# Hybrid pooling and SSD layer on one core: scan exponents and sample-state scaling on ScalarE, one state product on GpSimd, two output weights split in earlier stages

## The chip, the cores and the metric

The kernel runs on one core of a Trainium2 chip. The metric is device time in microseconds, from launch to the end of the last instruction, as the median of several executions. Times of single instructions come from one profiled execution of the kernel before, recorded by the hardware profiler. Engines are named as the profile names them: PE is TensorE (PEld its weight loads), DVE is VectorE, ACT is ScalarE, POOL is GpSimd, and SP is the queue of the engine that issues nearly all DMAs.

## The reference, cut to what matters

One layer of a decoder trunk: a SwiGLU FFN, a token mixing with two branches (multi-scale causal pooling and a Mamba-2 SSD scan, merged by gates), and a second SwiGLU FFN. There are 1024 prompt tokens and 8 x 8 sample tokens, D_MODEL 1024, D_FF 2816, 32 SSD heads of 64 channels in 4 groups, state 128, chunks of 128 tokens. All inputs are float32.

```python
def ssd_scan(x, dt, A, bm, cm, h0):
    ...
    a_cs = jnp.cumsum(dtr * A.reshape(G, R), axis=2)
    ...
    seg = jnp.where(causal, acs_t[..., :, None] - acs_t[..., None, :], -jnp.inf)
    decay = jnp.exp(seg)
    cb = jnp.einsum('bclgn,bcsgn->bcgls', cr, br)
    y_diag = jnp.einsum('bcgrls,bcsgrp->bclgrp', cb[:, :, :, None] * decay, xdt)
    ...
    def step(h, inp):
        s_c, d_c = inp
        return h * d_c[..., None, None] + s_c, h
    ...

def token_mixing(...):
    proj = hn @ w_in
    ...
    branch_pool = pool_mix(u_ext, T, out_pos0, pool_w_group, pool_scale) @ pool_w_out
    ...
    branch_ssd = y @ ssd_w_out
    gates = jax.nn.sigmoid(gate_logits.astype(f32)).reshape(Bsz, T, N_BRANCHES, D_MODEL)
    merged = (gates[:, :, 0] * branch_pool.astype(f32) + gates[:, :, 1] * branch_ssd.astype(f32)).astype(hn.dtype)
    return merged @ w_o, new_pool, new_conv, new_ssm
```

The decay is exp(a_l - a_s) on and below the diagonal of a chunk. Above the diagonal the exponent is positive and the result is multiplied by zero, so the kernel limits it to zero first.

## The kernel before

**Layout and precision.** Activations lie with channels on the 128 partitions and tokens along the row, in two halves: half 0 is 512 prompt tokens, half 1 is 512 prompt tokens and the 64 sample tokens. A float32 product is made of three passes over split operands, hi x hi, lo x hi and hi x lo, where hi is the operand rounded for the fast matmul and lo the rest. `split` (line 352) makes hi on ScalarE (line 354) and lo on VectorE (lines 356, 358). Weights come in chunks of 512 x 128 (256 KB).

**Weights.** `load_w` (line 270) loads a raw chunk (`wraw`, line 290), makes `wh` on ScalarE (293) and `wl` on VectorE (294). With `keep` it also stores both parts to DRAM (298), for half 1 to load them (283) without a split. `part` (line 304) is a generator that does the same ahead of time: it loads a chunk as `pr` (308), waits PART_W, splits it (354, 356), stores `ph` and `pr` (314, 315), waits PART_PACE, and takes the next one. `parted` holds what has been stored, and `load_w` looks there first. Before the change 52 chunks go through `part`: during FFN 1, twelve of its output weight, twelve of FFN 2's input weight and sixteen of w_o; during FFN 2, twelve of its output weight. `pool_w_out` (16 chunks) and `ssd_w_out` (32 chunks) are split in the mixing stage by half 0, with `keep`.

**Stages.** FFN 1 (to about 800 us of the span), the input projection (to 1510), the mixing stage (to 2220), FFN 2. FFN input and projection multiply pairs of weight tiles by the seven products of a Strassen-Winograd scheme (`wino`, line 466); each product is done for half 0 and half 1, its PSUM bank is read by ScalarE or VectorE and, for three of the four later products on that bank, is used again one product after. The sums of weights are made on GpSimd (436), their parts on ScalarE (442) and VectorE (443).

**The mixing stage** does, in this order on TensorE: pool branch of half 0 and of half 1 (`pgm`, `pbp`), then for each half the SSD output product group by group (`pso`), the merge, and the output projection (`pwo`). Beside them runs the scan as a generator, `scan`, through `ssd_group` for half 0 groups 0 to 3 and half 1 groups 0 to 3; a chunk is prepared by `ssd_a` (decay matrix `ab`, transposes), used by `ssd_b` one chunk later, and its state is made by `ssd_st`. Half 1 has a fifth chunk per group with the sample tokens, whose states `h` are loaded, transposed, updated and stored in 8 units per group.

**What sets the order.** Generators are called chains. Each `yield x` says that the chain continues when x more units have passed on `pe[0]`, a running estimate of TensorE's time in us, which is raised at every matmul as the program is written out. STEP is the distance between the steps of the scan for half 0 and half 1. Where an output is needed before its chain has come that far, `scanned` runs the chain on without waiting. The tile framework then orders the instructions of each engine and inserts the waits. Each engine executes its queue strictly in order, and so does SP with its DMAs: a store that waits for its data holds the loads behind it.

Of the kernel before, what the change touches and what calls it, by code (L numbers as in the profile page):

```python
# [12 lines left out]
ALU = mybir.AluOpType  # L13
# [29 lines left out]

STEP = (5.0, 4.0)
STEP_S = 1.0
# [10 lines left out]
HP, HP_ST = 40, 0  # L56
PART_AT, PART_W, PART_PACE = 20.0, 4.0, 3.0


@with_exitstack  # L60
def tile_hybrid_pool_ssd_macaron(
# [71 lines left out]
    def start(gen, delay=0.0):  # L133
        c = Chain(gen, delay)
        chains.append(c)
        return c
# [990 lines left out]
    def in_proj(prep):  # L1127
# [23 lines left out]
        c = poster[0] = start(worker())  # L1151
        work.append(sample_hist())
        for i in range(N_GATE[0], 16, 2):
            proj_pair("g", i, i + 1, both)
# [4 lines left out]
        ahead_d = []  # L1159
        for k in range(2):  # L1160
            ahead_d.append(load_d(0, k))
        for i in range(N_GATE[1], N_GATE[0], 2):
            proj_pair("g", i, i + 1, both[1:])
        last[0] = True
        for c_ in dts + [c]:
            finish(c_)
# [29 lines left out]
    out01 = [(kb, min(4, NFF - kb), m * P) for m in (0, 1) for kb in range(0, NFF, 4)]  # L1196

    def side():
        yield from part(ffn1_w_out[0], out01)
        yield from part(ffn2_w_in[0], [(kb, 4, c0 + ff * P) for ff in range(N_PLAIN[0]) for kb in (0, 4) for c0 in (0, FF)])  # L1200
        yield from part(w_o[0], [(kb, 4, m * P) for m in range(KD) for kb in (0, 4)])

# [19 lines left out]
    def pool_branch(h):  # L1222
# [20 lines left out]
        for m in range(KD):  # L1243
            t = act((P, N), name="t0")
            dma(t, gd[h][m])
            pb = dense(pool_w_out[0], 0, KD, m * P, [(h, fh, fl)], name="pbp", keep=True)[0]
            for pt, (a, b) in zip(pb, PIECES[h]):
# [38 lines left out]
    def ssd_a(h, g, c, Bf, Cf, xs4, dts):  # L1286
# [46 lines left out]
        for q, ab in enumerate(abs_):  # L1333
# [4 lines left out]
            for i in range(hq):  # L1338
                V.tensor_scalar(ab[:L, i, :], ab[:L, i, :], acs[:L, hc + q * hq + i : hc + q * hq + i + 1], 0.0,
                                op0=ALU.subtract, op1=ALU.min)  # L1340
            S.activation(ab[:L], ab[:L], AF.Exp)
            V.tensor_tensor(ab[:L], ab[:L], cbm[:L, :L].unsqueeze(1).broadcast_to([L, hq, L]), op=ALU.mult)
        return abs_, xp, xd, ea, btok, L, tok

    def ssd_b(h, g, c, a, hold, Cf, y4, dts):
# [8 lines left out]
        if smp:  # L1354
# [22 lines left out]
            for i, (pr, bh) in enumerate(units):  # L1377
                if i + 3 < len(units):
                    h0s[i + 3] = load(units[i + 3])
                hTs[pr], h0 = turn(h0s[i]), h0s.pop(i)  # L1380
                yield STEP_S
                gp = g * 4 + pr
                pn = psum("ps", "pnew")
                mm(pn, xd[bh][0][:, pr * P : (pr + 1) * P], xd[bh][1].rearrange("p b n -> p (b n)"))
                for b in range(4):
                    V.scalar_tensor_tensor(h0[:, b, :], h0[:, b, :], cdp[0][:, gp, bh * 4 + b : bh * 4 + b + 1],
                                           pn[:, b * P : (b + 1) * P], op0=ALU.mult, op1=ALU.add)
                dst = new_ssm_s[0, bh * 4 : bh * 4 + 4, 2 * gp : 2 * gp + 2].rearrange("b h p n -> (h p) b n")
# [34 lines left out]
    def ssd_st(h, g, c, a, dts):  # L1423
# [10 lines left out]
        with tc.high_priority(HP_ST):  # L1434
            if hold is None:
                S.copy(hn_, pst)
            else:
                V.tensor_tensor(hn_.rearrange("p (h d) -> p h d", d=HD), hold.rearrange("p (h d) -> p h d", d=HD),
                                cd[:, hc : hc + HPG].unsqueeze(2).broadcast_to([P, HPG, HD]), op=ALU.mult)
                V.tensor_tensor(hn_, hn_, pst, op=ALU.add)  # L1440
# [123 lines left out]
    def merge(h, acc):  # L1564
# [18 lines left out]
        for m in range(KD):  # L1583
            pb = dense(ssd_w_out[0], (NG - 1) * 4, 4, m * P, [yn], name="pso", keep=True)[0]
            while merged[0] <= m:
# [162 lines left out]
```

## Time and profile before

| | us |
|---|---|
| median of three timed runs | 2989.28 |
| lowest and highest of them | 2986.2, 2989.44 |
| the profiled execution | 2982.28 |
| its span, first to last instruction | 2980.5 |
| PE busy in the span | 2842.1 |
| mixing stage, 1520 to 2220 of the span: PE, VectorE, ScalarE, GpSimd busy | 624.9, 543.8, 267.2, 156.1 |

The mean granted clock of TensorE over the span is 0.982 of full speed. Times in the profile are us from the start of the span, durations in groups are ns. Matmuls are pipelined, so two can be counted as running at once, and a busy PE is not yet PE at its peak. A wait is put down to what ended last.

### The profile page before, as it was taken

Reading aid. Unit: us, or ns where it says so; the run is one execution under the profiler, and the core shown is the slowest. Engines: PE = TensorE matmul, PEld = TensorE weight load, DVE = VectorE, ACT = ScalarE, POOL = GpSimd, SP = SyncE. Lnnn points to the kernel's source line nnn. Section 1 sums busy time; section 2 is a strip of 40 time slices with the busy share of each in tenths; the row PEclk is TensorE's granted clock in tenths of the full one; section 3 lists DMA queues with packets and bytes.
Section 4 is the critical chain, followed back from the end, with each engine's and each line's share of the span. In section 5 each row is a group of like instructions: output and inputs, shape, how many; then the busy total and the mean of one; then the engine's idle time right before and its main releaser. Section 6 shows DMA issues by size and latency. Waiting matters only on the chain. (4 is left out here: it accounts for less than half of the span.)

```text
span 2980.5 us, 51010 instructions
## 1 busy us (share of the span) xinstructions
PE 2842.1 (95%) x18494; PEld 2580.8 (87%) x18494; DVE 1838.0 (62%) x3255; ACT 1264.6 (42%) x2592; POOL 963.4 (32%) x983
## 2 busy tenths in 40 slices
PE   7999999999999999999988998798999999999998
PEld 6999998789889989999876876577999999997898
DVE  6555556424564677696957798888666554453432
ACT  5444445323344555455543354334133444443422
POOL 5444444000233455464411221222125444440000
PEclk9999999999999999999998999899999999999999
DMA  4575554865343242323388888776674432236652
GB/s 133 162 225 180 173 159 149 270 192 177 100 124 110 88 136 87 125 96 119 109 277 285 280 266 253 231 248 196 226 244 157 155 110 80 77 94 220 210 161 73
DMA packets 521884, 503.78 MB, mean 169 GB/s; under 512 B 36628, under 2 KB 366216, under 8 KB 521624
## 3 DMA queue, kind: packets, MB, share of 16 engines
q1 hardware_dynamic: 521616, 500.52, 52.9%
q8 instruction: 145, 2.38, 0.3%
q14 instruction: 107, 0.88, 0.1%
q10 hardware_dynamic: 16, 0.00, 0.0%
HBM read 349.19 MB, written 151.44 MB: 168 GB/s over the span
## 5 line engine op out<-in xcount | busy, mean ns | idle before, releaser
L162 PE MATMUL pw<-X,wh 128*128 128x288 f32 (+1 forms) x2484 | 623.3, 330 | 13.7 <-ACT v L559 4.9
L162 PE MATMUL pw<-X,wl 128*128 128x288 f32 (+1 forms) x1644 | 472.8, 288 | 1.9 <-DVE wl L443 1.9
L162 PEld LDWEIGHTS pw<-X,wh 128*128 128x128 f32 x2484 | 418.1, 189 | 52.7 <-ACT v L559 5.8
L162 PE MATMUL pw<-hl,wh 128*128 128x512 f32 x1072 | 389.5, 398 | 1.1 <-DVE t L563 1.1
L443 DVE TENSOR_TENSOR wl<-s,wh 128x512 fp32r<-128x512 f32 x288 | 220.8, 767 | 213.6 <-ACT wh L442 192.5
L162 PE MATMUL pw<-hi,wh 128*128 128x288 f32 x1120 | 330.7, 295 | 1.0 <-ACT t L595 0.8
L162 PE MATMUL pw<-lo,wh 128*128 128x288 f32 x1120 | 329.7, 294 | 0.0
L162 PE MATMUL pw<-hi,wl 128*128 128x288 f32 x1120 | 329.6, 294 | 0.0
L294 DVE TENSOR_TENSOR wl<-wraw,wh 128x512 fp32r<-128x512 f32 x244 | 172.1, 707 | 253.4 <-ACT wh L293 247.5
L162 PEld LDWEIGHTS pw<-X,wl 128*128 128x128 f32 x1644 | 310.7, 189 | 2.5 <-DVE wl L443 2.5
L436 POOL TENSOR_TENSOR s<-wraw,wraw 128x512 f32<-128x512 f32 x144 | 204.3, 1418 | 314.1 <-DVE wl L443 223.5
L293 ACT ACTIVATE wh<-wraw 128x512 fp32r<-128x512 f32 x244 | 148.1, 609 | 365.7 <-PE po L162 239.2
L162 PE MATMUL pw<-hl,wl 128*128 128x256 f32 x1072 | 298.8, 279 | 1.2 <-DVE wl L443 1.2
L443 DVE TENSOR_TENSOR wl<-wraw,wh 128x512 fp32r<-128x512 f32 x216 | 163.9, 759 | 143.1 <-ACT wh L442 138.7
L442 ACT ACTIVATE wh<-s 128x512 fp32r<-128x512 f32 x288 | 181.1, 629 | 144.3 <-PE pw L162 141.6
L162 PEld LDWEIGHTS pw<-hl,wh 128*128 128x128 f32 x1072 | 201.2, 188 | 37.1 <-DVE t L563 1.4
L162 PEld LDWEIGHTS pw<-hi,wh 128*128 128x128 f32 x1120 | 210.0, 188 | 13.2 <-ACT t L595 1.6
L162 PE MATMUL po<-hh,wh 128*128 128x288 f32 (+1 forms) x800 | 210.6, 323 | 4.3 <-ACT hh L354 4.2
L162 PE MATMUL po<-hr,wh 128*128 128x288 f32 (+1 forms) x800 | 211.1, 323 | 0.2 <-DVE hr L356 0.2
L162 PE MATMUL po<-hh,wl 128*128 128x288 f32 (+1 forms) x800 | 210.6, 322 | 0.0
L162 PEld LDWEIGHTS pw<-lo,wh 128*128 128x128 f32 x1120 | 210.1, 188 | 0.0
L162 PEld LDWEIGHTS pw<-hi,wl 128*128 128x128 f32 x1120 | 210.1, 188 | 0.0
(383 smaller groups left out, 6256.1 us busy)
## 6 DMA issues: line engine op xcount, KB each, us to landing
wraw<-in_ffn_w_in_dram SPq DMA_DIRECT2D x188, 256.0 KB
wraw<-in_w_in_dram SPq DMA_DIRECT2D x144, 256.0 KB
wh<-part SPq DMA_DIRECT2D x140, 256.0 KB
wl<-part SPq DMA_DIRECT2D x140, 256.0 KB
wraw<-in_ffn_w_out_dram SPq DMA_DIRECT2D x120, 256.0 KB
ab<-acsd SPq DMA_DIRECT2D x64, 256.0 KB
hd<-g SPq DMA_DIRECT2D x44, 288.0 KB
part<-ph SPq DMA_DIRECT2D x48, 256.0 KB
```

The costliest lines, as they stand in the source:

```text
L162: T.matmul(out, lhsT, rhs, start=start, stop=stop, skip_group_check=free)
L293: S.activation(wh, raw, AF.Copy)
L294: V.tensor_tensor(wl, raw, wh.bitcast(F32), op=ALU.subtract)
L436: G.tensor_tensor(t, a, b, op=op)
L442: S.activation(wh, a, AF.Copy)
L443: V.tensor_tensor(wl, a, wh.bitcast(F32), op=ALU.subtract)
```

## The change

1. In `ssd_a` the clamp `min(ab - acs, 0)` per head on VectorE becomes `relu(-ab + acs)` on ScalarE with the sum as bias, and the exponential takes scale -1.
2. In `ssd_b`, for the sample states, ScalarE scales the four 128 x 128 blocks of `h` by the decay, and VectorE adds `pnew` in one instruction of 512 columns, in place of four fused instructions on VectorE.
3. In `ssd_st` the product of the running state and the chunk's decay goes from VectorE to GpSimd; the addition of `pst` stays on VectorE.
4. `pool_w_out` goes through `part` during FFN 1, after w_o; `ssd_w_out` goes through it during the projection, as a chain of its own that starts 2 units into it. The mixing stage asks for no `keep` any more, so both halves load stored parts.
5. `part` is started 6 units into an FFN's main loop, not 20, and its two waits are 2.5 and 1.5, not 4 and 3.
6. STEP goes from (5.0, 4.0) to (5.4, 4.3), and four d tile pairs of the pool branch, not two, are loaded at the projection's end.

```diff
-STEP = (5.0, 4.0)
+STEP = (5.4, 4.3)
...
-PART_AT, PART_W, PART_PACE = 20.0, 4.0, 3.0
+PART_AT, PART_W, PART_PACE = 6.0, 2.5, 1.5
...
         work.append(sample_hist())
+        split_so = start(part(ssd_w_out[0], so_chunks), 2.0)
...
-        for k in range(2):
+        for k in range(4):
             ahead_d.append(load_d(0, k))
...
-        for c_ in dts + [c]:
+        for c_ in dts + [split_so, c]:
             finish(c_)
...
+    so_chunks = [(g * 4, 4, m * P) for g in range(NG) for m in range(KD)]
...
-        yield from part(w_o[0], [(kb, 4, m * P) for m in range(KD) for kb in (0, 4)])
+        for w in (w_o[0], pool_w_out[0]):
+            yield from part(w, [(kb, 4, m * P) for m in range(KD) for kb in (0, 4)])
...
-            pb = dense(pool_w_out[0], 0, KD, m * P, [(h, fh, fl)], name="pbp", keep=True)[0]
+            pb = dense(pool_w_out[0], 0, KD, m * P, [(h, fh, fl)], name="pbp")[0]
...
             for i in range(hq):
-                V.tensor_scalar(ab[:L, i, :], ab[:L, i, :], acs[:L, hc + q * hq + i : hc + q * hq + i + 1], 0.0,
-                                op0=ALU.subtract, op1=ALU.min)
-            S.activation(ab[:L], ab[:L], AF.Exp)
+                S.activation(ab[:L, i, :], ab[:L, i, :], AF.Relu, bias=acs[:L, hc + q * hq + i : hc + q * hq + i + 1], scale=-1.0)
+            S.activation(ab[:L], ab[:L], AF.Exp, scale=-1.0)
...
                 hTs[pr], h0 = turn(h0s[i]), h0s.pop(i)
+                gp = g * 4 + pr
+                for b in range(4):
+                    S.activation(h0[:, b, :], h0[:, b, :], AF.Copy, scale=cdp[0][:, gp, bh * 4 + b : bh * 4 + b + 1])
                 yield STEP_S
...
-                for b in range(4):
-                    V.scalar_tensor_tensor(h0[:, b, :], h0[:, b, :], cdp[0][:, gp, bh * 4 + b : bh * 4 + b + 1],
-                                           pn[:, b * P : (b + 1) * P], op0=ALU.mult, op1=ALU.add)
+                hv = h0.rearrange("p b n -> p (b n)")
+                V.tensor_tensor(hv, hv, pn, op=ALU.add)
...
-                V.tensor_tensor(hn_.rearrange("p (h d) -> p h d", d=HD), hold.rearrange("p (h d) -> p h d", d=HD),
+                G.tensor_tensor(hn_.rearrange("p (h d) -> p h d", d=HD), hold.rearrange("p (h d) -> p h d", d=HD),
...
-            pb = dense(ssd_w_out[0], g * 4, 4, m * P, [yn], name="pso", keep=True)[0]
+            pb = dense(ssd_w_out[0], g * 4, 4, m * P, [yn], name="pso")[0]
```

Three places in the order of the engines' queues follow. A row has line, operation, out<-in and shape; x4 means four like it in a row.

ScalarE in the scan, in the SSD output of half 0, before. `ab` is half of a chunk's decay matrix, `ea` the decay of the old state, `btok` the transposed B, `acc` the sum of the SSD output:

```order
L1559 COPY acc_3575_19725<-pso_19683 128x512
L293 ACTIVATE wh_19872<-wraw_19871 128x512
L1321 COPY btok_19757<-pcb_19752 128x128
L1337 ACTIVATE ea_19764<-ab_19718 64x256 x2
L1337 ACTIVATE ea_19764<-ab_19720 64x256 x2
L1559 COPY acc_3591_19784<-pso_19727 128x512
L1341 ACTIVATE ab_19718<-ab_19718 128x512
L293 ACTIVATE wh_19931<-wraw_19930 128x512
L1341 ACTIVATE ab_19720<-ab_19720 128x512
```

The same place with the change (its lines are numbered up to four higher):

```order
L1563 COPY acc_3738_19906<-pso_19858 128x512
L1341 ACTIVATE ea_19937<-ab_19892 64x256
L1325 COPY btok_19930<-pcb_19925 128x128
L1341 ACTIVATE ea_19937<-ab_19892 64x256
L1343 ACTIVATE ab_19892<-ab_19892,dts_17889 128x128 x4
L1341 ACTIVATE ea_19937<-ab_19894 64x256
L1344 ACTIVATE ab_19892<-ab_19892 128x512
L1341 ACTIVATE ea_19937<-ab_19894 64x256
L1343 ACTIVATE ab_19894<-ab_19894,dts_17889 128x128 x4
L1563 COPY acc_3749_19962<-pso_19908 128x512
L1344 ACTIVATE ab_19894<-ab_19894 128x512
```

The weight's `wh` (L293) is gone from the queue, and two times four Relus (L1343) stand ahead of the exponentials (L1344).

SP in the SSD output of half 0, before, where `wraw` is a raw weight chunk and `part` the stored halves of one:

```order
L298 DMA part_20251<-wl_20246 128x512
L298 DMA part_20341<-wh_20336 128x512
L298 DMA part_20342<-wl_20337 128x512
L298 DMA part_20399<-wh_20394 128x512
L298 DMA part_20457<-wh_20452 128x512
L290 DMA wraw_20613<-in_ssd_w_out_dram 128x4x128
L290 DMA wraw_20651<-in_ssd_w_out_dram 128x4x128
L298 DMA part_20570<-wh_20565 128x512
L290 DMA wraw_20732<-in_ssd_w_out_dram 128x4x128
L1304 DMA ab_20286<-acsd_116 128x512
```

With the change:

```order
L283 DMA wh_20616<-part_11294 128x512
L283 DMA wl_20618<-part_11295 128x512
L283 DMA wh_20641<-part_11360 128x512
L283 DMA wl_20643<-part_11361 128x512
L1510 DMA bc_20439<-cv_21_165 128x576
L283 DMA wh_20727<-part_11434 128x512
L283 DMA wl_20729<-part_11435 128x512
L1308 DMA ab_20533<-acsd_116 128x512
L1308 DMA ab_20535<-acsd_116 128x512
```

No load stands behind a store of a weight any more; each chunk has two loads.

SP in FFN 1 beside the parts, before, where `pr` is a chunk to be split and `wraw` a chunk of the weight that is being multiplied:

```order
L308 DMA pr_4651<-in_w_o_dram 128x4x128
L462 DMA wraw_5078<-in_ffn_w_in_dram 128x4x128
L314 DMA part_4701<-ph_4698 128x512
L315 DMA part_4702<-pr_4651 128x512
L308 DMA pr_4749<-in_w_o_dram 128x4x128
L462 DMA wraw_5080<-in_ffn_w_in_dram 128x4x128
L314 DMA part_4798<-ph_4795 128x512
L315 DMA part_4799<-pr_4749 128x512
L462 DMA wraw_5082<-in_ffn_w_in_dram 128x4x128
L462 DMA wraw_5323<-in_ffn_w_in_dram 128x4x128
```

With the change:

```order
L308 DMA pr_3274<-in_w_o_dram 128x4x128
L462 DMA wraw_3719<-in_ffn_w_in_dram 128x4x128
L314 DMA part_3311<-ph_3308 128x512
L315 DMA part_3312<-pr_3274 128x512
L308 DMA pr_3342<-in_w_o_dram 128x4x128
L308 DMA pr_3411<-in_w_o_dram 128x4x128
L314 DMA part_3377<-ph_3374 128x512
L315 DMA part_3378<-pr_3342 128x512
L462 DMA wraw_3721<-in_ffn_w_in_dram 128x4x128
L314 DMA part_3447<-ph_3444 128x512
L315 DMA part_3448<-pr_3411 128x512
L462 DMA wraw_3723<-in_ffn_w_in_dram 128x4x128
```

Between two loads of `wraw` there is now up to a whole chunk of `pr` with its two stores, and some loads of `pr` stand ahead of the stores of the chunk before.

More of the change, by code (lines that the diff above doesn't have):

```diff
@@ L1380, in ssd_b @@
                 hTs[pr], h0 = turn(h0s[i]), h0s.pop(i)
+                gp = g * 4 + pr
+                for b in range(4):
+                    S.activation(h0[:, b, :], h0[:, b, :], AF.Copy, scale=cdp[0][:, gp, bh * 4 + b : bh * 4 + b + 1])
                 yield STEP_S
-                gp = g * 4 + pr
                 pn = psum("ps", "pnew")
                 mm(pn, xd[bh][0][:, pr * P : (pr + 1) * P], xd[bh][1].rearrange("p b n -> p (b n)"))
-                for b in range(4):
-                    V.scalar_tensor_tensor(h0[:, b, :], h0[:, b, :], cdp[0][:, gp, bh * 4 + b : bh * 4 + b + 1],
-                                           pn[:, b * P : (b + 1) * P], op0=ALU.mult, op1=ALU.add)
+                hv = h0.rearrange("p b n -> p (b n)")
+                V.tensor_tensor(hv, hv, pn, op=ALU.add)
                 dst = new_ssm_s[0, bh * 4 : bh * 4 + 4, 2 * gp : 2 * gp + 2].rearrange("b h p n -> (h p) b n")
@@ L1583, in merge @@
         for m in range(KD):
-            pb = dense(ssd_w_out[0], (NG - 1) * 4, 4, m * P, [yn], name="pso", keep=True)[0]
+            pb = dense(ssd_w_out[0], (NG - 1) * 4, 4, m * P, [yn], name="pso")[0]
             while merged[0] <= m:
```

## The prediction

> **What bounds the kernel now.** I read the busy shares first, then the windows by stage, then in the worst stage who waits for whom. The page's first part gives each engine's share of the span:
>
> ```profile
> PE 2842.1 (95%) x18494; PEld 2580.8 (87%) x18494; DVE 1838.0 (62%) x3255; ACT 1264.6 (42%) x2592; POOL 963.4 (32%) x983
> ```
>
> TensorE sets the time, so a gain can only come where it idles. The windows (PE, PEld, DVE, ACT and POOL busy us, granted clock, DMA share, GB/s): first FFN 1, the projection's gate part and its first convolutions, and FFN 2 with part tiles; then the mixing stage whole and in five pieces.
>
> ```profile
> core 0: us, PE busy (x) PEld busy (x) DVE busy (x) ACT busy (x) POOL busy (x), PEclk, DMA share, GB/s
> 100.00:500.00 400.00, 398.74 (x2695) 375.12 (x2694) 226.70 (x377) 188.38 (x414) 176.70 (x167) 1.00 0.56 177
> 860.00:1020.00 160.00, 160.00 (x1095) 150.29 (x1094) 80.69 (x138) 75.35 (x151) 59.87 (x64) 1.00 0.34 102
> 1020.00:1100.00 80.00, 77.89 (x516) 72.06 (x516) 70.86 (x117) 43.71 (x95) 45.13 (x53) 1.00 0.40 128
> 1520.00:1600.00 80.00, 61.62 (x301) 45.23 (x300) 51.77 (x108) 30.76 (x61) 13.78 (x10) 0.88 0.91 300
> 1600.00:1740.00 140.00, 133.61 (x917) 118.65 (x916) 109.97 (x241) 60.36 (x127) 28.74 (x23) 0.96 0.85 280
> 1740.00:1960.00 220.00, 187.55 (x1132) 141.29 (x1130) 192.25 (x403) 90.70 (x182) 55.95 (x46) 0.94 0.79 250
> 1960.00:2040.00 80.00, 66.65 (x451) 54.18 (x452) 64.38 (x155) 33.10 (x70) 17.82 (x15) 0.88 0.67 214
> 2040.00:2220.00 180.00, 175.48 (x1386) 168.86 (x1386) 125.45 (x239) 52.30 (x100) 39.83 (x32) 1.00 0.72 235
> 2310.00:2410.00 100.00, 98.85 (x662) 92.74 (x661) 55.14 (x88) 46.13 (x98) 47.08 (x44) 1.00 0.50 157
> ...
> 1520.00:2220.00 700.00, 624.91 (x4180) 528.21 (x4179) 543.81 (x1144) 267.22 (x538) 156.13 (x125) 0.94 0.78 254
> ```
>
> FFN 1 idles 1.3 us in 400. The mixing stage idles 75.1 in 700 and pays again through the clock: PE busy times (1 - clock) is 7.4, 5.3, 11.3, 8.0 and 0 us in the five pieces, 32 together. Idle plus clock by piece: 25.8 (pool branch, half 0; DMA share 0.91), 11.7 (pool, half 1), 43.7 (SSD output, half 0; VectorE 87% busy), 21.4 and 4.5. That is all there is to win here, some 107 us.
>
> The view of waits (who waits, for whom: us in total, times, longest) names the causes. TensorE's in the third piece:
>
> ```profile
> PE pst L162 <- DVE xd L1329: 4.2, 4, 2.5
> ...
> PE pso L162 <- DVE wl L294: 3.3, 3, 1.1
> PE pso L162 <- ACT wh L293: 3.2, 2, 2.7
> ```
>
> Those of SP's own queue, over the whole stage:
>
> ```profile
> SPq L283 <- PE pso L162: 92.9, 31, 15.5
> SPq L298 <- ACT wh L293: 47.4, 23, 6.5
> SPq L298 <- DVE wl L294: 44.3, 25, 12.5
> ```
>
> And one such wait in the timeline (start and length in us, in brackets the idle time before it and what ended it):
>
> ```profile
> 1843.90 0.32 SPq L298 DMA_DIRECT2D part<-wl  x1
> ...
> 1844.75 2.39 SPq L290 DMA_DIRECT2D wraw<-in_ssd_w_out_dram  x4
> ...
> 1849.21 0.63 ACT L293 ACTIVATE wh<-wraw 128x512 fp32r<-128x512 f32 x1 [1.91 <-DMA wraw<-in_ssd_w_out_dram]
> ...
> 1849.89 2.08 PE L162 MATMUL pso<-yhl,wh 128*128 128x512 f32 x4 [2.69 <-ACT wh L293]
> ```
>
> SP issues in order. The store of a split weight (L298) stands until VectorE has made it, the raw loads (L290) stand behind it, so ScalarE gets its chunk late and TensorE stops 2.69 us. So three things press on this stage at once: VectorE's time, SP's order and the bytes.
>
> **The change part by part.** The groups that price it, by line and shape (out<-in, count | busy us, mean ns of one | idle before, and what ended it):
>
> ```profile
> L1339 DVE TENSOR_SCALAR ab<-ab,dts 128x128 f32<-128x128 f32 x256 | 59.4, 295 | 10.0 <-ACT ea L1337 8.6
> ...
> L1339 DVE TENSOR_SCALAR ab<-ab,dts 64x64 f32<-64x64 f32 x32 | 6.2, 242 | 0.3
> ...
> L294 DVE TENSOR_TENSOR wl<-wraw,wh 128x512 fp32r<-128x512 f32 x56 | 42.5, 764 | 10.6 <-ACT wh L293 9.6 <-DMA wraw<-in_pool_w_out_dram 1.0
> ...
> L1386 DVE SCALAR_TENSOR_TENSOR h<-h,cdp,pnew 128x128 f32<-128x128 f32 x128 | 35.1, 344 | 10.5 <-PE pnew L162 8.5 <-issue 1.1 <-PE ph0T L166 0.8
> ...
> L1438 DVE TENSOR_TENSOR hst<-hst,dts 128x512 f32<-128x512 f32 x28 | 20.4, 729 | 0.0
> ...
> L1440 DVE TENSOR_TENSOR hst<-hst,pst 128x512 f32<-128x512 f32 x28 | 19.1, 683 | 1.6 <-PE pst L162 1.3
> ...
> L1321 ACT COPY btok<-pcb 128x128 f32<-128x128 f32 x32 | 8.4, 262 | 72.6 <-DVE cbm L1317 72.2 <-DMA d<-dh 0.4
> ...
> L1337 ACT ACTIVATE ea<-ab 64x256 f32<-64x256 f32 x136 | 56.4, 415 | 40.7 <-DMA ab<-acsd 38.4
> ...
> L932 ACT ACTIVATE ct<-ra,cols 128x512 f32<-128x512 f32 x24 | 19.7, 819 | 38.1 <-POOL ra L1116 38.1
> ...
> L354 ACT ACTIVATE ph<-pr 128x512 fp32r<-128x512 f32 x48 | 30.3, 631 | 29.2 <-DMA pr<-in_w_o_dram 12.1 <-DMA pr<-in_ffn_w_out_dram 9.4 <-DMA pr<-in_ffn_w_in_dram 7.5
> ...
> L356 DVE TENSOR_TENSOR pr<-pr,ph 128x512 fp32r<-128x512 f32 x48 | 39.4, 821 | 41.9 <-ACT ph L354 38.8 <-DMA part<-ph 1.2 <-issue 0.6
> ...
> L1331 POOL TENSOR_TENSOR xs<-xs,Dcol 128x512 f32<-128x512 f32 x32 | 38.5, 1203 | 182.6 <-PE pxT L166 147.4 <-DMA bc<-cv 29.4 <-DVE xs L1491 5.7
> ```
>
> VectorE in the mixing stage loses the exponent clamps (59.4 + 6.2), 48 of the 56 weight splits (48 x 0.764 = 36.7), the state product (20.4), and in the sample states 35.1 against 32 adds of the kind of L1440 (21.9): 135.9 us of 543.8. ScalarE gains a Relu per head. No row shows one; L1321 (0.262, same 128x128, no operand by partition) bounds it below, L1337 (0.415) above. L932 has two operands by partition and takes 0.188 more than L354's plain 128x512, so one costs 0.094 and I take 0.356: 288 Relus 102.5 us, 128 scalings 45.6, less 48 splits of 0.631 (30.3): +118 (75 to 142), so 385 of 700. A chunk of the scan, one per 19.4 us (700 / 36), needs about 6 us of it; that lies beside TensorE's dense matmuls, and the decay matrix is read a chunk later. Without that cover TensorE would wait up to those 6 us a chunk, 36 times. GpSimd gains 28 products of 1.203 (L1331 has the same broadcast form), 34 of its 544 idle us. The new wait is VectorE's add of pst on that product; behind it stand adds of pso that free PSUM. In the program's order the product precedes the xs sum on GpSimd and needs only the last state, so it should be there first: nothing. At worst each add waits one product, 28 x 1.203 = 34 us of VectorE.
>
> A product on GpSimd can hold VectorE up:
>
> ```profile
> 1839.97 3.35 POOL L1482 TENSOR_TENSOR xs<-xs,z 128x576 f32<-128x576 f32 x2
> ...
> 1841.99 1.88 DVE L294 TENSOR_TENSOR wl<-wraw,wh 128x512 fp32r<-128x512 f32 x1
> ```
>
> VectorE's subtraction, started at 1841.99, ends 0.55 us after GpSimd's at 1843.32. The Trainium skill (SBUF — State Buffer, Who interferes with whom) says that a VectorE instruction with two SBUF inputs and a GpSimd one that reads SBUF exclude each other for a whole instruction; by that rule, which the trace bears out here, the worst case is another 34 us of VectorE, and I would put the sum some 5 us later (an estimate).
>
> DMA: the 96 stores of 256 KB leave the stage, and half 0 loads two parts instead of one raw chunk, 48 loads more: net 48 x 0.262 = 12.6 MB of 178 MB less, 4.2 MB of them in the pool branch. At 300 GB/s that is 14 us of the first piece, and four d tiles (1 MB) loaded a stage earlier are 3.5. Everything that SP waited for at L298, 91.7 us, goes; what is late next is the buffer that TensorE has to free, the wait L283 has already.
>
> By piece I expect back: 14 of 25.8 in the first (the transfers), 4 of 11.7 in the second, 27 of 43.7 in the third (VectorE from 87% to about 62%, SP's queue free; the short chains through merge and rstd stay), 5 of 21.4 in the fourth, where the first group of half 1 is still run without pacing when its output is due, 0 in the last: 50 us. The longer STEP spreads the scan: 71% of the dense matmul columns stand ahead of its last piece now, 79% then. I count that inside the 50.
>
> The same splits come back earlier: 48 more part chunks (16 in FFN 1, 32 in the projection), each a load, L354, L356 and two stores, and all 100 follow each other faster. FFN 1 hid 40 of them at a cost of at most 1.3 us. ScalarE and VectorE have room there (0.63 and 0.82 us per chunk, against half-idle engines), except in 1020:1100, where VectorE is 89% busy and some 9 chunks add 7.4 us to 9.1 us of slack: I take 4. What can go wrong is the queue:
>
> ```profile
> 323.96 0.48 SPq L308 DMA_DIRECT2D pr<-in_ffn_w_in_dram  x1
> ...
> 328.19 0.63 ACT L354 ACTIVATE ph<-pr 128x512 fp32r<-128x512 f32 x1 [2.44 <-DMA pr<-in_ffn_w_in_dram]
> ```
>
> A load takes 4.2 us to land, and ScalarE stood 2.44 us for it. The split now follows the load after 2.5 units of the pacer in place of 4, so this happens oftener. TensorE's slack for a late ScalarE is about one of the seven products with both halves, since the bank that ScalarE copies is needed again one product later: 20 matmuls at 0.148 us (2695 in 400 us), 3 us. I take 6 us over the three stages: 2 in FFN 1, 3 in the projection, 1 in FFN 2. Bounds: 0, and 100 x 1.2 us = 120.
>
> **Sum.** -50 + 4 + 6 = -40. The profiled execution took 2982.28 (span 2980.5 and 1.8 around it): 2942. The three timed runs have their median 7.0 above it, so the forecast is **2949**.
>
> **Rivals.** (1) *TensorE-bound throughout*: the stage comes to the 97 to 100% of the projection and the clock stays up. Of the 107 us, 85 come back, 5 are paid: 2982.3 - 80 + 7 = 2909. For it: no engine but PE is then over 65%. Against: the chains through merge, rstd and the state loads are untouched. (2) *The queue of the parts*, slower: in the program's order seven chunks now stand on two tile pairs of FFN 1 (five before), so one comes every 5.9 us (14 products of 3 us by seven), where load, split and stores one behind the other need 4.2 + 0.63 + 0.82 and two issues of 0.32, 6.3 us. What ScalarE loses beyond TensorE's slack is paid 100 times; from 0.5 us per chunk on it eats the 50. At 0.75: 2982.3 - 50 + 4 + 75 + 7 = 3018. Against: FFN 1's 40 chunks cost nothing, and 32 of the 100 loads stand in SP's order ahead of the stores of the chunk before. (3) *Transfers bound the stage anyway*: share 0.79 to 0.91, 7% less to move; then only some 10 of the 50 come, 10 are paid: 2989, no change.
>
> **How the numbers follow.** Forecast 0.62, (1) 0.16, (2) 0.13, (3) 0.09. The forecast's own range is 2930 to 2975. The range takes in (3) and half of (1): 2912 to 2992; left out are (2) and the rest of (1). 0.2% (6 us) is about what a measurement of this kernel can tell from no change. Faster 0.78, same 0.09, slower 0.13.
>
> **What would show it.** Right: the mixing stage near 650 us with PE clock near 0.98; VectorE near 410 us in it; no wait of SP on a split there; the windows 100:500 and 860:1100 with under 10 us of PE idle. Wrong: waits of ScalarE for pr over 100 us with PE idle in FFN 1 and the projection (rival 2), VectorE waiting for GpSimd's hst, or a DMA share over 0.9 through the pool and SSD pieces (rival 3).

## The result and the profile after

The changed kernel took **2972.75 us** (median of 5 runs, 2965.9 to 2977.94), the kernel before 2987.71 (5 runs, 2985.98 to 2989.44): ratio 0.995, interval 0.9932 to 0.9967. That is 15 us less, where 40 were forecast from the profiled run; the time, 24 us above the forecast of 2949, lies inside the forecast's range of 2912 to 2992. The profiled run of the changed kernel took 2975.98 (span 2974.2), so against the profiled run of before (2982.28) only 6.3 us less: the one lies 3.2 above its median, the other 5.4 below the median of the later runs. The stage by stage comparison that follows is of these two runs and adds up to 6.3; the 9 us between that and 15 can't be given to a stage.

The page's first part, after:

```profile
PE 2838.9 (95%) x18494; PEld 2579.6 (87%) x18494; DVE 1763.4 (59%) x2843; ACT 1374.6 (46%) x3008; POOL 989.6 (33%) x1011
```

VectorE lost 74.6 us, ScalarE gained 110, TensorE does the same 18494 matmuls and is no less busy. Cut at the last matmul of each stage (FFN 1's gate half, which is all of it ahead of its first output matmul; its output half; the projection; the mixing stage; FFN 2), the windows of before are

```profile
0.00:526.00 526.00, 502.06 (x3296) 465.96 (x3297) 313.91 (x516) 258.54 (x572) 242.76 (x255) 0.99 0.54 170
526.00:792.00 266.00, 263.97 (x1600) 240.59 (x1599) 103.01 (x163) 78.40 (x132) 9.25 (x11) 1.00 0.62 193
792.00:1516.00 724.00, 708.17 (x4663) 658.13 (x4663) 523.21 (x871) 373.25 (x768) 339.80 (x390) 1.00 0.37 114
1516.00:2218.00 702.00, 626.82 (x4189) 529.83 (x4188) 543.96 (x1143) 268.96 (x540) 156.13 (x125) 0.94 0.79 254
2218.00:2980.00 762.00, 741.04 (x4754) 686.31 (x4753) 353.92 (x564) 285.46 (x582) 215.45 (x203) 0.99 0.42 134
```

and of after

```profile
0.00:540.00 540.00, 506.16 (x3300) 468.47 (x3301) 331.83 (x533) 262.96 (x588) 241.09 (x256) 0.99 0.60 189
540.00:806.00 266.00, 263.53 (x1596) 240.30 (x1595) 103.21 (x162) 78.48 (x131) 8.97 (x11) 1.00 0.62 192
806.00:1541.00 735.00, 712.61 (x4666) 660.23 (x4665) 550.45 (x903) 392.01 (x800) 342.62 (x390) 0.99 0.47 147
1541.00:2205.00 664.00, 611.26 (x4186) 520.97 (x4186) 428.21 (x683) 355.50 (x908) 183.57 (x153) 0.97 0.77 249
2205.00:2974.00 769.00, 745.30 (x4755) 689.67 (x4753) 349.71 (x564) 285.61 (x582) 213.41 (x203) 0.99 0.42 133
```

Both runs have the same number of matmuls in each stage to within a few, so the lengths compare directly:

| us | before | after | difference | forecast |
|---|---|---|---|---|
| FFN 1, gate half | 526.4 | 539.9 | +13.5 | +2 |
| FFN 1, output half | 265.7 | 266.1 | +0.4 | 0 |
| projection | 724.4 | 735.1 | +10.7 | +7 |
| mixing stage | 701.6 | 664.0 | -37.6 | -50 |
| FFN 2 | 762.4 | 769.1 | +6.7 | +1 |

So the mixing stage gave three quarters of what was forecast for it, and the chunks that were split earlier took back 31 us where 10 were forecast. In the mixing stage SP has no store of a split weight to stand at any more (91.7 us before); what it waits for is the buffer that TensorE frees (after; 92.9 us before):

```profile
SPq L283 <- PE pso L162: 155.7, 51, 11.0
```

In FFN 1's gate half ScalarE's waits for the raw chunk of a part were 24.3 us before, over 40 chunks,

```profile
ACT ph L354 <- DMA pr<-in_w_o_dram: 12.1, 6, 3.7
ACT ph L354 <- DMA pr<-in_ffn_w_in_dram: 7.5, 4, 2.6
ACT ph L354 <- DMA pr<-in_ffn_w_out_dram: 4.7, 3, 2.5
```

and are 78.8 after, over 56 chunks, with a longest of 4.4:

```profile
ACT ph L354 <- DMA pr<-in_pool_w_out_dram: 25.8, 9, 4.3
ACT ph L354 <- DMA pr<-in_w_o_dram: 25.0, 9, 4.4
ACT ph L354 <- DMA pr<-in_ffn_w_in_dram: 17.2, 8, 3.6
ACT ph L354 <- DMA pr<-in_ffn_w_out_dram: 10.8, 5, 3.1
```

TensorE's new waits there are for VectorE's copies and for the input rows (after; before, none at that copy and 0.2 us for the rows):

```profile
PE pw L162 <- DVE t L563: 5.2, 6, 1.6
PE ptr L166 <- DMA xin<-in_x_prompt_dram: 4.6, 3, 2.2
```

FFN 2 shows one whole case. SP's queue and ScalarE's around the first part chunk (timelines of after; in brackets the idle time ahead and what ended it):

```profile
2271.59 0.43 SPq L308 DMA_DIRECT2D pr<-in_ffn_w_out_dram  x1
2278.71 0.37 SPq L462 DMA_DIRECT2D wraw<-in_ffn_w_in_dram  x1
```

```profile
2272.13 0.38 ACT L593 COPY t<-pw 128x288 f32<-128x288 f32 x1
2276.92 0.63 ACT L354 ACTIVATE ph<-pr 128x512 fp32r<-128x512 f32 x1 [4.41 <-DMA pr<-in_ffn_w_out_dram]
2277.46 0.61 ACT L442 ACTIVATE wh<-wraw 128x512 fp32r<-128x512 f32 x1
2277.98 0.38 ACT L595 COPY t<-pw 128x288 f32<-128x288 f32 x1
```

The chunk's load goes out at 2271.59, its split stands at the head of ScalarE's queue until 2276.92, and behind it stands L595, the copy that frees TensorE's bank. TensorE's wait and the clock of that stretch (after; the waits of 2205 to 2300, and the window):

```profile
PE pw L162 <- ACT t L595: 3.6, 1, 3.6
```

```profile
2266.00:2297.00 31.00, 26.51 (x168) 25.01 (x167) 14.80 (x21) 13.14 (x27) 15.42 (x13) 0.89 0.51 154
```

Before, the same stretch, 13 us later, ran at full clock:

```profile
2279.00:2310.00 31.00, 29.68 (x209) 28.35 (x208) 19.51 (x24) 13.96 (x29) 17.98 (x14) 1.00 0.43 132
```

3.6 us of wait and 2.9 us of clock (26.51 x 0.11) make up FFN 2's 6.7 nearly alone; matmul by matmul, the step at this place is 6.1 us.

### The profile page after: what moved, and what is told of

It reads as the page before. It is cut to its first block, busy times and chain, and to the rows that moved or that the text cites. A ratio compares the mean times of both kernels' runs of the same rounds, so it can differ in the third digit from the quotient of the medians.

```text
span 2974.2 us, 51139 instructions
## 1 busy us (share of the span) xinstructions
PE 2838.9 (95%) x18494; PEld 2579.6 (87%) x18494; DVE 1763.4 (59%) x2843; ACT 1374.6 (46%) x3008; POOL 989.6 (33%) x1011
## 5 line engine op out<-in xcount | busy, mean ns | idle before, releaser
L294 DVE TENSOR_TENSOR wl<-wraw,wh 128x512 fp32r<-128x512 f32 x196 | 136.3, 696 | 246.0 <-ACT wh L293 231.2
L293 ACT ACTIVATE wh<-wraw 128x512 fp32r<-128x512 f32 x196 | 117.8, 603 | 299.5 <-PE po L162 224.5
L443 DVE TENSOR_TENSOR wl<-wraw,wh 128x512 fp32r<-128x512 f32 x216 | 169.7, 786 | 121.1 <-ACT wh L442 114.0
```

Source lines behind the costliest of these rows:

```text
L293: S.activation(wh, raw, AF.Copy)
L294: V.tensor_tensor(wl, raw, wh.bitcast(F32), op=ALU.subtract)
L443: V.tensor_tensor(wl, a, wh.bitcast(F32), op=ALU.subtract)
```

## The experiments

After the result the open questions were what the early chunks cost by (their pace, their number, or the engine that they load) and which part of the change had gained in the mixing stage. All times are medians; each ratio is to runs of the kernel before on the same chip. Where two kernels are compared matmul by matmul, it is the start of the n-th of the 18494 matmuls in each.

The runs were made on several chips, on which the kernel before has medians of 2986.6 to 2988.3 us, so times of kernels from different chips can be off by a us or two against each other. Stages are read from one profiled execution of each kernel, and these scatter: the six kernels below whose projection has the same code and pace take 729.6 to 736.7 us for it, and the six kernels with the same mixing stage (the changed one among them) 658.1 to 664.0.

### The old pace

The changed kernel with one line put back:

```
-PART_AT, PART_W, PART_PACE = 6.0, 2.5, 1.5
+PART_AT, PART_W, PART_PACE = 20.0, 4.0, 3.0
```

> The changed kernel with the part chunks at the old pace (start 20, then 4 and 3 units a chunk). Stages of the changed kernel against before, by their last TensorE instructions: FFN 1's first half 526 to 540 us, projection 724 to 735, mixing 701 to 664, FFN 2 763 to 769. Theory A (pace: the split follows its load too closely, ScalarE stands for the load, and SP's store and TensorE's copies behind it): FFN 1's first half falls to 528 to 531, projection to 725 to 730, FFN 2 to 763; mixing stays at 664; time 2950 to 2956. Theory B (number: 48 more chunks with their loads, stores and ScalarE and VectorE work cost, however spaced): FFN 1's first half stays at 536 or more, the projection at 733 or more, FFN 2 763; time 2963 to 2970.

Measured: 3000.76 us (6 runs, 2996.98 to 3003.83), ratio 1.0045 (1.0029 to 1.0061): slower than before. Neither theory has this. Matmul by matmul FFN 1 runs 1 to 2 us ahead of before up to 520 us. By the end of the half 46 chunks are split, 40 before, so six more chunks at that pace cost nothing, as theory A says. Then it loses 47 us at one place, the end of the gate half (window and TensorE's wait):

```profile
526.00:573.00 47.00, 0.49 (x1) 0.29 (x1) 16.37 (x25) 14.00 (x23) 1.00 (x2) 0.52 0.91 299
```

```profile
PE po L162 <- ACT hh L354: 47.8, 1, 47.8
```

The stage ends by finishing the chain of parts, and ten of its 56 chunks were still to do. Two of them in ScalarE's timeline:

```profile
544.00 0.63 ACT L354 ACTIVATE ph<-pr 128x512 fp32r<-128x512 f32 x1 [3.09 <-DMA pr<-in_pool_w_out_dram]
544.71 0.63 ACT L354 ACTIVATE hh<-hr 128x512 fp32r<-128x512 f32 x1
549.23 0.63 ACT L354 ACTIVATE ph<-pr 128x512 fp32r<-128x512 f32 x1 [3.89 <-DMA pr<-in_pool_w_out_dram]
```

One behind the other they take some 4.7 us each (47 / 10), and FFN 1's output half waits behind them. So 56 chunks at 7 units don't fit into the gate half, where 40 did: the faster pace, which the prediction treated as a cost only, was needed. The projection (738 us) and the mixing stage (661.7) stay as in the changed kernel.

### Each half of the change alone

The kernel before with the three moves off VectorE only (the lines of the diff for L1339, L1386 and L1438):

> The kernel before with only the moves off VectorE (Relu on ScalarE, state scaling on ScalarE, state product on GpSimd); weight splits, pace and STEP as before. Theory A (the mixing stage gained by SP's queue and the bytes): the mixing stage keeps 690 us or more of 701, time 2978 to 2990. Theory C (it gained by VectorE's time): mixing 670 to 685, time 2958 to 2972. FFN 1, projection and FFN 2 as before in both (526, 724, 763).

Measured: 2983.94 us (12 runs, 2977.81 to 2992.8), ratio 0.9989 (0.9976 to 1.0002); mixing stage 705 us against 702:

```profile
1516.00:2222.00 706.00, 638.78 (x4191) 538.09 (x4189) 466.53 (x732) 381.29 (x956) 187.61 (x153) 0.93 0.78 252
```

VectorE is 77 us less busy than before. TensorE idles 67 us, 75 before, but its clock is no better (0.93, 0.94 before) and the stage is no shorter. Theory C falls: these moves bring nothing here. One rival is left: with them VectorE waits 35.3 us for the Exp ahead of its product with the mask (1.8 before), and that the longer chain through ScalarE ate a gain of VectorE's time is not excluded.

The kernel before with the parts only, at the old pace:

```
+        split_so = start(part(ssd_w_out[0], so_chunks), 2.0)
...
-        yield from part(w_o[0], [(kb, 4, m * P) for m in range(KD) for kb in (0, 4)])
+        for w in (w_o[0], pool_w_out[0]):
+            yield from part(w, [(kb, 4, m * P) for m in range(KD) for kb in (0, 4)])
...
-            pb = dense(ssd_w_out[0], g * 4, 4, m * P, [yn], name="pso", keep=True)[0]
+            pb = dense(ssd_w_out[0], g * 4, 4, m * P, [yn], name="pso")[0]
```

> The kernel before with only the pool and scan output weights split earlier (16 chunks more in FFN 1, 32 in the projection, at the old pace, no storing of splits in the mixing stage); VectorE's work there as before but for the splits. Theory A (SP's queue and the bytes): mixing 670 to 678, FFN 1's first half 528 to 531, projection 725 to 730, time 2958 to 2968. Theory C (VectorE's time): mixing 685 to 695, time 2976 to 2986. Theory B of the pace run (number of chunks) would show here as FFN 1's first half at 536 or more and the projection at 733 or more.

Measured: 3023.65 us (6 runs, 3019.73 to 3026.81), ratio 1.0121 (1.0103 to 1.0138), with the same 50 us lost at the end of FFN 1's gate half (577 us). The mixing stage came to 680:

```profile
1581.00:2261.00 680.00, 623.66 (x4184) 531.98 (x4184) 514.82 (x1095) 241.81 (x491) 156.56 (x125) 0.95 0.75 243
```

22 us of the 38 thus come with the splits and their stores gone from the stage, between the forecasts of theory A (670 to 678) and theory C (685 to 695) and nearer to A. SP's queue, the bytes and the splits' own time on VectorE (29 us, 544.0 to 514.8) go in one edit here and are not told apart. The moves bring nothing by themselves; 16 us of the whole change's gain are still without an owner.

### The load one chunk ahead

The changed kernel at its own pace, with the next chunk's load issued ahead of this chunk's split:

```
+        ts = {0: raw(0)}
+        yield PART_W
+        for i, (k0, nk, c0) in enumerate(chunks):
+            if i + 1 < len(chunks):
+                ts[i + 1] = raw(i + 1)
+            t = ts.pop(i)
...
-            yield PART_PACE
+            yield PART_PACE + PART_W
```

> The changed kernel at its own pace (2.5 and 1.5 units, start at 6), but each chunk's load is issued one chunk earlier, so that some 6 us lie between load and split instead of some 4. Theory A (ScalarE standing for the load): its waits for pr in FFN 1 fall from 68 us to under 15, FFN 1's first half to 528 to 532, projection 726 to 730, FFN 2 763 to 766, time 2952 to 2960. Theory B (number of chunks, or too many in a short time): the waits for pr go too, but FFN 1's first half stays at 536 or more and the time within 5 us of 2973.

Measured: **2952.58 us** (6 runs, 2951.55 to 2964.28), ratio 0.9891 (0.9872 to 0.9909), 20 us less than the changed kernel (18 by the ratios) and less than both. FFN 1's gate half fell to 528.1, and ScalarE's waits for pr in it from 78.8 to 14.4 us (the lines of this kernel are numbered eight higher):

```profile
ACT ph L362 <- DMA pr<-in_pool_w_out_dram: 7.2, 4, 3.1
ACT ph L362 <- DMA pr<-in_ffn_w_in_dram: 3.3, 4, 1.8
ACT ph L362 <- DMA pr<-in_w_o_dram: 3.3, 4, 1.2
...
ACT ph L362 <- DMA pr<-in_ffn_w_out_dram: 0.6, 2, 0.3
```

The chunks, their number and their deadline are those of the changed kernel. From load to split it is now 5.8 us in FFN 1 (median, 4.6 before this edit), and in SP's queue the load stands ahead of the stores of the chunk before. The chunks also follow each other faster, every 5.0 us in place of 6.4, though the units are the same: a chain goes on at the first check after its units have passed, and a chunk now has one such stop, not two. The faster pace speaks against theory B, so most of FFN 1's cost is ScalarE standing for a load that was just issued, with SP's order behind it, as theory A says. Not all of it: counted from the first chunk on (110 us), the changed kernel loses 13.7 us against before up to the end of the gate half, and this one still 4.2 (it is 2.6 us ahead of before at that point). The other kernels below with the load ahead lose 3.6 to 7.1.

In the projection the edit takes no wait away (28.2 us for pr, 20.7 in the changed kernel), and the stage stays at 734.6 us.

### The start, the spacing and the engine

The first two edits are made on the load-ahead kernel, the third on the one that comes of the first. First the start put back to 20 units:

```
-PART_AT, PART_W, PART_PACE = 6.0, 2.5, 1.5
+PART_AT, PART_W, PART_PACE = 20.0, 2.5, 1.5
```

> The load-ahead kernel (2952.6 us; FFN 1's first half 528, projection 735, mixing 659, FFN 2's first half 480 us) with the parts started 20 units after FFN's start, as before the change, in place of 6. Theory D (the 5 us that FFN 2 lost lie at its first chunk, whose load ScalarE waits for while TensorE needs its copies): FFN 2's first half back to 475, FFN 1's first half 526 to 528, time 2945 to 2949. Theory B (they are the chunks' own work, wherever they start): FFN 2 stays at 480, time 2950 to 2955.

Measured: 2954.08 us (4 runs, 2950.72 to 2955.96), ratio 0.9891 (0.9874 to 0.9908). FFN 2's gate half is 473.6 us (480.2 with start 6, 475.9 before): the step of 6 us at its first chunk, which has no chunk ahead of it and so no early load, is gone, as theory D says. It holds beyond these two: with the load ahead, the kernels that start at 6 take 478.3 to 480.2, the three that start at 20 take 473.6 to 474.2. The medians don't show it: 2954.1 and 2952.6 can't be told apart, and theory D's 2945 to 2949 is missed.

Then the projection's chunks spread over the stage (the new argument is the distance of two chunks in units):

```
-        split_so = start(part(ssd_w_out[0], so_chunks), 2.0)
+        split_so = start(part(ssd_w_out[0], so_chunks, 11.0), 2.0)
```

> The load-ahead kernel with the projection's 32 chunks spread over the whole stage, one every 11 units in place of 4 (some 17 us for 6.2). Theory E (the projection's 10 us are lost because VectorE is nearly full where the convolutions begin and the chunks stand closest there): projection 726 to 729, time 2944 to 2949. Theory B (each chunk costs its 0.3 us wherever it stands): projection stays at 733 or more, time 2950 to 2955.

Measured: 2958.13 us (6 runs, 2952.36 to 2963.38), ratio 0.9906 (0.9888 to 0.9923); projection 735.4. ScalarE's waits for pr, 28.2 us in the projection at 4 units, are none at 11, and still the stage loses as much; matmul by matmul most of the loss now comes in steps between 1060 and 1500 us instead of before 1110. Theory E falls. The spacing does not matter in any kernel: with a chunk every 4.7 us (load ahead), 6.3 (changed), 9.5 (old pace) and 13.7 (here) the projection takes 734.6, 735.1, 738.3 and 735.4 us. So a chunk costs TensorE some 0.3 us there (10.2 / 32) wherever it stands, give or take the scatter of the stage.

And their subtraction on GpSimd:

```
-            V.tensor_tensor(lo, src, hi.bitcast(F32), op=ALU.subtract)
+            (eng or V).tensor_tensor(lo, src, hi.bitcast(F32), op=ALU.subtract)
```

> The load-ahead kernel started at 20 (2954.1 us; projection 734, FFN 2's first half 474), with the subtraction of the projection's 32 chunks on GpSimd in place of VectorE (32 x 0.82 us off VectorE there, 32 x some 1.2 on to GpSimd). Theory J (the projection's 10 us are what the chunks take of VectorE): projection 726 to 729, time 2946 to 2950. Theory K (they are ScalarE's copies, or the transfers): projection 732 or more, time 2951 to 2958.

Measured: 2960.07 us (4 runs, 2956.7 to 2963.44), ratio 0.991 (0.9898 to 0.9923); projection 742.8, so worse by 8 us, and by 6 than the slowest of the kernels with the same pace. The stretch of the chunks in the kernel with start 20, and here:

```profile
935.00:1070.00 135.00, 130.99 (x857) 122.33 (x856) 100.64 (x153) 80.60 (x161) 63.51 (x74) 0.97 0.70 224
```

```profile
940.00:1085.00 145.00, 134.59 (x862) 122.11 (x861) 94.19 (x133) 78.27 (x159) 93.32 (x97) 0.99 0.66 208
```

GpSimd's busy share goes from 47 to 64%, and TensorE takes 9 us more for the same matmuls, counted matmul by matmul. Theory J is not borne out, and GpSimd is no free place; whether VectorE's or ScalarE's share of a chunk is what the projection pays stays open.

### STEP, the early d tiles and the moves

Which part owns the rest of the mixing stage's gain? The load-ahead kernel without the three moves:

> The load-ahead kernel with the three moves off VectorE undone (exponent clamps, sample state scaling and state product back on VectorE); the parts, STEP and the four early d tiles stay. Theory F (the moves are worth something once the splits are gone, since the parts alone brought the mixing stage to 680 and all together to 662): mixing 672 to 680, time 2966 to 2974. Theory G (the moves are worth nothing, as alone on the kernel before, 705 against 702, and the 18 us came from STEP and the d tiles): mixing 657 to 663, time 2951 to 2957.

Measured: 2960.02 us (6 runs, 2953.29 to 2964.5), ratio 0.991 (0.9892 to 0.9927); mixing 665.0, between the two forecasts and nearer to theory G. So the moves are worth 7 us at most (by the medians; 6.4 by the stage), and that is not clear of noise: the intervals of the two ratios overlap, and kernels with the moves reach 664.0. And with the moves, but STEP and the d tiles put back:

```
-STEP = (5.4, 4.3)
+STEP = (5.0, 4.0)
...
-        for k in range(4):
+        for k in range(2):
```

> The load-ahead kernel with STEP back at 5.0 and 4.0 and two early d tiles in place of four; the moves stay. Theory F (the moves): mixing 657 to 665, time 2950 to 2960. Theory G (STEP and the d tiles): mixing 674 to 680, time 2967 to 2975.

Measured: 2977.59 us (12 runs, 2972.06 to 2986.09), ratio 0.9969 (0.9957 to 0.998); mixing 682.0, so theory G and not F. STEP alone put back:

> The load-ahead kernel (2952.6 us, mixing 659) with only STEP back at 5.0 and 4.0; four early d tiles stay. With STEP and the d tiles both put back it was 2977.6, mixing 682. Theory H (STEP alone): mixing 676 to 684, half-clock time in it near 70 us as then (34 with the longer STEP), time 2968 to 2978. Theory I (the early d tiles): mixing 657 to 665, time 2950 to 2958.

Measured: 2975.41 us (5 runs, 2968.92 to 2979.23), ratio 0.9961 (0.9949 to 0.9973); mixing 677.6. Theory H holds: the two numbers of STEP are worth some 21 to 23 us here (by the ratios and by the medians). What the d tiles add, 2 us by the medians, can't be told from noise. The mixing stage of the load-ahead kernel, without the moves, and with the old STEP:

```profile
1528.00:2187.00 659.00, 611.03 (x4187) 521.46 (x4185) 426.46 (x683) 355.34 (x907) 184.96 (x153) 0.97 0.77 251
```

```profile
1529.00:2195.00 666.00, 611.48 (x4190) 524.66 (x4188) 510.13 (x1096) 243.93 (x492) 156.10 (x125) 0.97 0.76 249
```

```profile
1525.00:2203.00 678.00, 623.01 (x4187) 531.87 (x4185) 427.20 (x683) 355.04 (x907) 190.07 (x153) 0.95 0.75 244
```

Between the first two rows VectorE's busy time differs by 84 us, and the granted clock is 0.97 in both; with the old STEP it is 0.95. TensorE's busy time times (1 - clock) is 18 us in the first row and 31 in the last, the idle time 48 and 55.

Is STEP worth that by itself? The kernel before with nothing but the longer STEP:

> The kernel before with nothing but STEP at 5.4 and 4.3. Theory H1 (STEP spreads the scan over more dense matmuls and is worth as much by itself): mixing 678 to 688 of 702, time 2964 to 2974. Theory H2 (it is worth something only when the splits and their stores are gone from the stage, since SP's and VectorE's waits hold the scan back else): mixing 695 to 703, time 2980 to 2990.

Measured: 2989.98 us (11 runs, 2984.26 to 2996.45), ratio 1.0015 (1.0006 to 1.0023); mixing 708.6. Cut at the first SSD output and the first w_o matmul, the stage of before and of this kernel:

```profile
1516.00:1722.00 206.00, 180.34 (x1130) 151.94 (x1129) 146.64 (x312) 83.27 (x169) 39.35 (x30) 0.93 0.86 284
1722.00:1907.00 185.00, 156.64 (x917) 117.90 (x915) 166.56 (x345) 83.35 (x169) 47.81 (x40) 0.94 0.78 250
1907.00:2218.00 311.00, 289.83 (x2146) 259.99 (x2147) 230.75 (x488) 102.33 (x202) 68.97 (x56) 0.96 0.74 236
```

```profile
1516.00:1724.00 208.00, 175.09 (x1096) 149.84 (x1096) 139.00 (x292) 77.39 (x157) 32.79 (x26) 0.92 0.84 278
1724.00:1875.00 151.00, 140.28 (x774) 108.58 (x772) 133.04 (x273) 68.07 (x137) 41.31 (x30) 0.95 0.80 259
1875.00:2225.00 350.00, 313.07 (x2321) 275.99 (x2321) 273.09 (x579) 124.27 (x247) 85.17 (x69) 0.95 0.72 232
```

The middle piece is 34 us shorter with 143 matmuls less in it, and the last one 39 longer with 175 more: the scan was only moved. Theory H2 holds in its direction, and the stage is even longer than its 703: a longer STEP gains only with the parts (mixing stage 677.6 to 658.6 with the parts; 701.6 to 708.6 without). Which of the things that go with the splits it needs, SP's queue or VectorE's waits, is not shown.

And STEP longer once more, on the kernel with start 20:

```
-STEP = (5.4, 4.3)
+STEP = (5.8, 4.6)
```

> The load-ahead kernel started at 20 (2954.1 us, mixing 659) with STEP at 5.8 and 4.6, as much again. If the scan is still packed too closely (half-clock time left in the stage: 34 us): mixing 648 to 656, time 2943 to 2951. If the dense matmuls now run out before the scan does: the last groups are run without cover, the stage from its first w_o product on grows from 332 us, mixing 662 or more, time 2957 or more.

Measured: 3003.89 us (6 runs, 2993.61 to 3007.82), ratio 1.0051 (1.0036 to 1.0066), 50 us slower than with 5.4. Its last piece:

```profile
1850.00:2242.00 392.00, 336.38 (x2433) 289.95 (x2433) 248.55 (x391) 200.85 (x519) 102.48 (x84) 0.91 0.66 209
```

392 us against 332 with 5.4: TensorE idles 56 us in it and runs at 0.91. The dense matmuls that can run without the scan's next output run out before the scan does, and that part of it has no cover: for 43 us, from 2110 to 2154, and for 27 before that TensorE has the scan alone (with 5.4 the longest such stretch is 7.6). Most of the longer one, in which it is busy 25 of 42 us:

```profile
2111.00:2153.00 42.00, 24.76 (x208) 16.81 (x206) 23.76 (x42) 29.00 (x81) 6.32 (x6) 0.80 0.54 154
```

The value of STEP has an edge right behind it.

## Why the prediction was wrong

**The parts: the step that failed.** The prediction took 6 us for the queue of the parts, "2 in FFN 1, 3 in the projection, 1 in FFN 2", and 4 more in 1020:1100; measured were 31.3. The mechanism was there as rival (2), at the wrong price on both sides: the queue was put at 0.06 us a chunk in the forecast and 0.75 in the rival, and the chunks cost 0.31 each. The argument was that FFN 1 hid 40 chunks at 1.3 us and that TensorE has 3 us of slack for a late ScalarE. The 40 were hidden at 7 units, and at 7 units 46 of the 56 are hidden as well (the old-pace run). At 4 units ScalarE stands up to 4.4 us, longer than that slack, and what it holds up is more than TensorE's banks: VectorE's copies come later, and TensorE waits 4.6 us for the input rows. The prediction had seen the wait itself (2.44 us in one case) and that it would come oftener, but took the slack to cover nearly all of it; for the rest it counted a split by its busy time (0.63 us), where its place in ScalarE's order, behind a load just issued, was the cost.

What the runs show of the cause: in FFN 1 issuing the load earlier takes back some 7 to 10 of 13.7 us; in FFN 2 another start of the first chunk takes back its 6; in the projection, a third of the 31, neither ScalarE's waits nor the spacing accounts for the loss, and the cause stays open. The mark that the prediction set for rival (2) was nearly met: ScalarE waits for pr 99.5 us in FFN 1 and the projection (over 100 was named), 109.8 with FFN 2, and TensorE idles 15.6 us in the windows 100:500 and 860:1100, 3.4 before.

**The deadline was not seen.** The prediction counted the pace as risk only. The old-pace runs show the other side: at 7 units ten chunks are left over and cost 47 us. The prediction's cadence (one chunk per 5.9 us) was about right: ScalarE's splits stand 6.4 apart in FFN 1.

**The projection.** Forecast 4 + 3, measured 10.7; by the n-th matmul 8.7 of them between 1020 and 1100 us, where the convolutions begin and 4 were forecast: place right, size a little low. The reason given, that VectorE is full there, isn't shown: spread out, the chunks cost the same.

**The first two pieces of the mixing stage.** 14 + 4 forecast; the way to the first SSD output is 20.1 us shorter (205.8 to 185.7). The size is right, the reason about half: with the parts alone it is 10.7 shorter (195.1), and STEP put back in the load-ahead kernel takes 9.7 away again (183.5 to 193.2). The longer STEP leaves some 34 matmuls fewer in this piece (1130 before, 1135 with the parts alone, 1096 after), so a part of the 20 is work that was moved behind it. That the sum came out was partly luck.

**The later pieces: right sign, wrong reason, 14 us too much.** 27 + 5 were forecast from VectorE (87% to 62%) and SP's queue; measured were 17.5 (495.8 to 478.3). VectorE fell as forecast (in the stage 544 to 428 us, forecast about 410), but the moves that took most of it alone gained nothing, and 7 us at most beside the rest. In these pieces the parts alone bring 10.8 us (495.8 to 485.0), and STEP in the load-ahead kernel 9.3 (484.4 to 475.1). STEP, which the prediction counted "inside the 50", carries some 19 us of the whole stage together with the parts (677.6 to 658.6). In the changed kernel part of what is won in the third piece is given back in the last: 41 us less before the first w_o product, 23 more after it.

**Terms of the moves.** In the stage after the change:

```profile
L1343 ACT ACTIVATE ab<-ab,dts 128x128 f32<-128x128 f32 x256 | 81.9, 391 | 1.6
...
L1386 ACT ACTIVATE h<-h,cdp 128x128 f32<-128x128 f32 x128 | 41.8, 397 | 17.7 <-PE ph0T L166 17.7
...
L1442 POOL TENSOR_TENSOR hst<-hst,dts 128x512 f32<-128x512 f32 x28 | 31.8, 1135 | 0.9 <-issue 0.9
...
L1444 DVE TENSOR_TENSOR hst<-hst,pst 128x512 f32<-128x512 f32 x28 | 19.1, 682 | 9.0 <-POOL hst L1442 6.0 <-PE pst L162 1.9 <-DMA z<-zd 0.4
```

A Relu takes 0.391 us (0.356 assumed), a scaling 0.397, the product on GpSimd 1.135 (1.203), and VectorE waits 6.0 us for it where nothing was forecast and 34 was the bound. ScalarE's busy time grew by 86.5 us, not 118: 256 Relus of 0.391 take 81.9 us of it, less than their durations' sum of 100, since they overlap. The chain through ScalarE did grow: VectorE waits 42.4 us for the Exp ahead of the mask product at L1345 (1.8 before). The kernel without the moves is no faster, so the moves as a whole did no visible harm; what that wait takes off their gain is not shown.

**Transfers.** Rival (3) let some 10 of the 50 us come because transfers bound the stage anyway; 37.6 came, at a DMA share of 0.77 (0.79 before). It falls. Rival (1) falls too: what it asked for is there, no engine but TensorE is over 65% in the stage, and the stage still idles 53 us.

## What to carry to other kernels

A load, its split and its store that are put into the order of engines with work of their own must stand far apart: issue the load one piece ahead, so that nothing waits for it at the head of a queue (here 18 to 20 us), and check that all pieces still fit before the seam that waits for them (here 47 us). An engine at 87% need not be what holds the stage: undo its load alone before giving it the gain, and try a pacing constant together with the edit that it is meant for, since alone it gained nothing here.

## What the runs showed of the hardware beside that

TensorE's clock cost half as much as its idle time: in the mixing stage before, 75 us idle went with 38 us lost at a clock of 0.94 (626.82 x 0.06). With the parts in, the kernels differ in this clock with the spread of the scan (0.95 over the stage with STEP at 5.0, 0.97 at 5.4, 0.93 at 5.8) and not with VectorE's busy time (0.97 at 426 us and at 510).

VectorE's product with the mask got slower with the moves, 0.721 us before and 0.805 after:

```profile
L1345 DVE TENSOR_TENSOR ab<-ab,cbm 128x512 f32<-128x512 f32 x64 | 51.5, 805 | 42.4 <-ACT ab L1344 42.4
```

With the moves alone it is 0.822, in the load-ahead kernel 0.789 and without them 0.701. From 0.721 to 0.805 it is 5 us of VectorE. The rule of the Trainium skill that the prediction weighed (SBUF — State Buffer, Who interferes with whom) agrees with it, since this product has two SBUF inputs and GpSimd has one more reader; that it is GpSimd's product, and not one of ScalarE's, is argued and not shown.
